# Odd layer: values stored by feature half, gate multiplied in the projection, sums of two heads at once, first projection tile emitted early; linear attention's second pass in backward order

## Chip, core and metric

The kernel runs on one core of a Trainium2 chip. The metric is the device time of one execution in microseconds (us). Before the change it is 3762.51 us, the median of 3 runs (3760.75 to 3772.91).

The core has TensorE (PE) for matrix products into PSUM, VectorE (DVE), ScalarE (ACT), GpSimd (POOL), and SyncE (SP), which here issues nearly all DMAs. Every engine works through its own queue in order. Where an instruction waits, all behind it on that engine wait too, the DMAs that SP or POOL are to issue included.

## What is computed

Two layers over 2048 latent tokens (a grid of 32 rows by 64 columns) and 256 context tokens, width 1024, in fp32. Layer 0 (even) has two branches, layer 1 (odd) has one:

```python
# layer 0: latent attention, 8 heads of 96 (values 64), keys = latents + context
s = q @ k.T * scale ; p = softmax(s) ; a = p @ v
# and gated linear attention, 4 heads, scanned over chunks in both directions
o = q_t @ state + att @ v ; state = state * decay + k_dec.T @ v
y = concat([a * silu(za), rms_norm(b) * silu(zb)]) @ w_out
# layer 1: neighbourhood attention, 16 heads of 64, window 8 rows x 16 columns
s = concat([q @ k_window.T * scale + bias, q @ k_ctx.T * scale])
o = softmax(s) @ concat([v_window, v_ctx])
y = (o * silu(z)) @ w_out
x = x + gate * y
```

## The kernel before

**Products.** fp32 operands are split into a high and a low fp32r part. A product is three matmuls: high x high, low x high, high x low (L114, L115, L116 in the projections; L961 to L963 in the even scores). L106 is the helper that every ACT instruction goes through.

**Stages**, by the trace: projections and row maxima of layer 0 to 1128 us; even attention with the linear attention woven into it, 1128 to 1993; projection 0 (18 tiles of 128 tokens) to about 2240; the four projections of layer 1 (`odd_qk`, `odd_vz`) to 3120; odd attention, 3120 to 3563; projection 1 (16 tiles) to the end, 3763.5.

**Even attention** (`even_attention`) runs 4 pairs of heads. For a block of up to 512 queries, it takes 18 key tiles of 128: scores on PE, exp on ACT into `apt`, `apt` times values on PE (L893). The sum of `apt` over the key tiles, the softmax's denominator before its last sum over partitions, is added up elementwise in `acc` (L952): two in five key tiles on POOL, the others on DVE, and L971 adds the two sums.

**Linear attention** (`gla`) has a first pass over 18 chunks, two scans (forward on POOL, tag gsf; backward on DVE, tag gsb: chunks 1, 0, then 17 down to 2, L788 to L790, three instructions for a chunk), and a second pass (L795 to L820) over chunks 0 to 17. The second pass multiplies the queries with the scanned states `D` (L804), adds, normalizes, transposes and copies the result with ACT into a tile of the tag gsb, which has two buffers and is also the scan's. `weave` puts its instructions into even attention's at a fixed ratio. When all is issued, the states' memory takes the split weights of projection 0 (the list `places`).

**Odd attention** (`odd_attention`) runs 8 pairs of heads j. For a pair, SP loads the queries (q, four tiles and a mask row), the context's keys (kc), two bias tables (tab; POOL adds the mask to each, L1338), the values V, and the latents' keys in four groups g of 512 tokens (kt), each ahead of its use. The two query sets of a pair are in fixed buffers, so that pair j+1's can be loaded when PE is through with pair j-1. Steps of a pair are c0, c1 (context keys for query blocks 0, 1), g0, c2, g1, c3, g2, g3. A group is four column tiles: scores (L1342, L1343), bias added on DVE from PSUM into `opt` (L1451), exp in place on ACT, then, some steps later, `opt` times values into the PSUM tile o (L1383; L1368 for context keys). The denominators are added up in `oacc`, per head: for context keys with a DVE reduce (L1374), for latent tiles with an add on POOL, for tiles 2 and 9 on DVE (L1391). `finish` sums over partitions on PE (L828), inverts on ACT and DVE, multiplies o by it (L835), multiplies by the gate z on POOL (L836; z is loaded by L1396), and a DMA of POOL's queue stores the block into RT1.

V is stored by POOL's DMAs (`store_v`) as 8 blocks of rows, one per residue of the grid row modulo 8. `values(j)` loads it back with one DMA for context rows (V1c) and eight for latents, of 16 partitions each: the 128 keys of a tile are in the order c, r, b (c: column group of 16, r: row modulo 8, b: column within 16), and so are K1t and the bias tables.

**Projection 1** (`project`): per tile, rows of RT (128 x 1024), hi on ACT, lo on DVE (L1066), 48 matmuls, gate (L1074) and residual (L1075). Its weights come in pair 7 in 16 chunks of 128 x 512 through one staging buffer (wraw, L375), are split by ACT and DVE (L378), and are placed in buffers that pairs 6 and 7 have left. Rows of tiles 0 and 1 are requested in between; PE takes their matmuls in the order in which the weights come.

The added instructions take their place on an engine from the order of emission, which `weave`, `issue_after` and a list of late steps move; nothing is planned by costs but the weave's ratio.

Of the kernel before, what the change touches and what calls it, by code (L numbers as in the profile page):

```python
# [17 lines left out]
P = 128  # L18
# [70 lines left out]
class Kern:  # L89
# [569 lines left out]

    def gla(self, gp, gs, g1, gd, pp, tag):  # L660
# [133 lines left out]
        scan(list(range(NCT - 1, -1, -1)) + list(range(NT - 1, NCT - 1, -1)), slice(64, 128), nc.vector, "gsb")  # L794
        for c in range(NT):  # L795
# [27 lines left out]
    def finish(self, av, dacc, zt, dst, w, ap, pp, tag, lnp=None, bufs=(1, 2), out=None):  # L823
# [12 lines left out]
        nc.gpsimd.tensor_tensor(out=rc[:, :w], in0=rc[:, :w], in1=zt, op=ALU.mult)  # L836
        (out or nc.sync).dma_start(dst, rc[:, :w])

    def even_attention(self, ap, pp):
# [71 lines left out]
        early, sums = {}, {}  # L911
        for j in range(4):
# [12 lines left out]
            for nb, (q0, w, kts) in enumerate(blocks):  # L925
# [8 lines left out]
                acc = [[None, None], [None, None]]  # L934
                first = [[None, None], [None, None]]

                def add(n, pts):
                    for i in range(2):
                        e = 1 if len(kts) > 2 and n % 5 in (1, 3) else 0
                        eng = nc.gpsimd if e else nc.vector  # L940
                        if acc[i][e] is None:
                            if first[i][e] is None:
                                first[i][e] = pts[i]
                                continue
                            if len(kts) == 2:
                                acc[i][e] = self.tl(ap, [P, CTX], f"accc{i}", bufs=1)
                            else:
                                acc[i][e] = self.tl(ap, [P, 512], f"acc{i}{e}", bufs=2 - e)
                            a = first[i][e]
                        else:  # L950
                            a = acc[i][e]
                        eng.tensor_tensor(out=acc[i][e][:, :w], in0=a[:, :w], in1=pts[i][:, :w], op=ALU.add)  # L952

                for n, kt in enumerate(kts):
# [13 lines left out]
                    if n == len(kts) - 1:  # L968
                        for i in range(2):
                            if acc[i][1] is not None:  # L970
                                nc.vector.tensor_tensor(out=acc[i][0][:, :w], in0=acc[i][0][:, :w], in1=acc[i][1][:, :w], op=ALU.add)  # L971
                        sums[j, nb] = [acc[i][0][:, :w] for i in range(2)]
# [19 lines left out]
    def even_mix(self, e1, win, hT):  # L992
# [3 lines left out]
        with ExitStack() as es:  # L996
            with ExitStack() as esa:
# [13 lines left out]
                places = [(g1, t) for t in ("gG", "gqt", "gkt", "gkT", "gat", "tri")] + [(gd, f"D{c}") for c in range(NT)]  # L1011
# [28 lines left out]
            self.project(0, self.RT, list(range(NT)), self.i["xin"], self.x1, w, sp, pp, ld, pre, ahead())  # L1040
# [4 lines left out]
    def project_load(self, RT, t, o, xsrc, ld):  # L1045
        r = self.tl(ld, [P, KD, P], "pr")
        self.nc.sync.dma_start(r[:], RT[:, :, o * P : o * P + P].rearrange("j p t -> p j t"))
# [4 lines left out]
    def project(self, l, RT, tiles, xsrc, dst, w, sp, pp, ld, pre, ahead=iter(())):  # L1052

        nc = self.nc
        gate = {}
        for c in range(2):
            if l == 0 or c == 0:
                gate[c] = self.tl(sp, [P, D], f"gate{c}", bufs=1)
                nc.sync.dma_start(gate[c][:], self.gates[l, c : c + 1].partition_broadcast(P))
        for t in tiles:  # L1060
            o = (t - tiles[0]) * P
            r, x = pre.pop(t) if t in pre else self.project_load(RT, t, t - tiles[0], xsrc, ld)
            hi = self.tl(sp, [P, KD, P], "prh", F32R)
            lo = self.tl(sp, [P, KD, P], "prl", F32R)
            self.act(hi[:], r[:])
            nc.vector.tensor_tensor(out=lo[:], in0=r[:], in1=hi[:], op=ALU.subtract)  # L1066
            g = gate[1 if t < NCT else 0]
            for n in range(2):
                c = slice(n * 512, n * 512 + 512)
                ps = self.tl(pp, [P, 512], "pj", bufs=4)  # L1070
                self.mm3(ps[:], (lambda k: hi[:, k, :], lambda k: lo[:, k, :]),
                         (lambda k: w[k, n][0][:, 0, :], lambda k: w[k, n][1][:, 0, :]), range(KD))
                y = self.tl(sp, [P, 512], "py")
                nc.vector.tensor_tensor(out=y[:], in0=ps[:], in1=g[:, c], op=ALU.mult)  # L1074
                nc.gpsimd.tensor_tensor(out=x[:, c], in0=y[:], in1=x[:, c], op=ALU.add)  # L1075
            nc.sync.dma_start(dst[o : o + P, :], x[:])
            next(ahead, None)
# [11 lines left out]
    def odd_qk(self, ws, win, hT):  # L1089
        nc = self.nc  # L1090
        self.V1c = self.scr("V1c", (P, NCT, D), F32)
        self.V1 = self.scr("V1", (8, 256, D), F32)
# [3 lines left out]
        with ExitStack() as es:  # L1096
# [8 lines left out]
            def cell(t, j):  # L1105
# [9 lines left out]
                if j == 4:  # L1115
                    n = self.tl(sp, [P, 512], "onat", bufs=4)
                    self.act(n[:], ps[:].rearrange("p h d -> p (h d)"))
                    self.store_v(t, slice(0, 512), n)
                    return
# [10 lines left out]
            def fin(t, j, n):  # L1130
# [24 lines left out]
                for r in range(2):  # L1155
                    oh, ol = (x[:].rearrange("p i (c r b) -> p i r c b", c=4, r=8)[:, :, r0 + r] for x in kt[j])
# [25 lines left out]
    def store_v(self, t, c, v):  # L1182

        if t < NCT:
            self.nc.gpsimd.dma_start(self.V1c[:, t, c], v[:])
            return
        g, a = divmod(2 * (t - NCT), 8)
        for r in range(2):
            self.nc.gpsimd.dma_start(self.V1[a + r, g * 64 : g * 64 + 64, c], v[r * 64 : r * 64 + 64])

    def odd_vz(self, ws, win, hT):
# [4 lines left out]
        with ExitStack() as es:  # L1196
# [6 lines left out]
            def cell(t, j):  # L1203
# [6 lines left out]
                if j < 6:  # L1210
                    self.act(n[:], ps[:])
                    self.store_v(t, slice((j - 4) * 512, (j - 3) * 512), n)
                    return
# [70 lines left out]
    def odd_attention(self, ld, right, wout):  # L1284
# [4 lines left out]
        with ExitStack() as es:  # L1289
# [51 lines left out]
            def scores(ps, k1, k2, q1, q2):  # L1341
                nc.tensor.matmul(ps, k1, q1, start=True, stop=False)  # L1342
                return nc.tensor.matmul(ps, k2, q2, start=False, stop=True)  # L1343

            mk = None
            pend, late = [], []
            for j in range(8):
# [15 lines left out]
                def tail_ctx(n, pts, j=j, V=V, O=O, acc=acc):  # L1363
# [6 lines left out]
                    for i in range(2):  # L1370
                        if n % 2 == 0:
                            acc[n // 2, i] = self.tl(rp, [P, 16, 64], f"oacc{n // 2}{i}", bufs=1)
                        a = acc[n // 2, i][:].rearrange("p r c -> p (r c)")[:, (n % 2) * 512 : (n % 2) * 512 + 512]
                        nc.vector.tensor_reduce(out=a, in_=pts[i][:].rearrange("p u c -> p c u"), axis=AX.X, op=ALU.add)  # L1374

                def tail(n, pts, j=j, V=V, O=O, acc=acc):
# [3 lines left out]
                    for bb in range(r0 // 8, (r0 + nr - 1) // 8 + 1):  # L1380
                        a0, a1 = max(r0, bb * 8), min(r0 + nr, bb * 8 + 8)
                        for i in range(2):
                            nc.tensor.matmul(O[bb][i * 64 : i * 64 + 64, a0 - bb * 8 : a1 - bb * 8, c0 : c0 + w],  # L1383
                                             V[:, NCT + n, i * 64 : i * 64 + 64], pts[i][:, a0 - r0 : a1 - r0, :],
                                             start=False, stop=bb in done, skip_group_check=True)
                    for hf in range(r0 // 16, (r0 + nr - 1) // 16 + 1):
                        a0, a1 = max(r0, hf * 16), min(r0 + nr, hf * 16 + 16)
                        for i in range(2):
                            a = acc[hf, i][:, a0 - hf * 16 : a1 - hf * 16, c0 : c0 + w]
                            eng = nc.vector if n in (2, 9) else nc.gpsimd  # L1390
                            eng.tensor_tensor(out=a, in0=a, in1=pts[i][:, a0 - r0 : a1 - r0, :], op=ALU.add)  # L1391
                    late.extend([2 + u, finish_block, bb, j, O, acc] for u, bb in enumerate(done))

                def finish_block(bb, j, O, acc):
                    zt = self.tl(fp, [P, 512], "ozt", bufs=3)
                    nc.sync.dma_start(zt[:], self.z1[j, :, bb * 512 : bb * 512 + 512])  # L1396
                    a = [acc[bb // 2, i][:].rearrange("p r c -> p (r c)")[:, (bb % 2) * 512 : (bb % 2) * 512 + 512] for i in range(2)]
                    self.finish(O.pop(bb)[:].rearrange("p r c -> p (r c)"), a, zt[:],
                                self.RT1[j, :, bb * 512 : bb * 512 + 512], 512, fp, pp, ("st", 4), lp, (2, 3), nc.gpsimd)

                def weights():

                    for k in range(KD):
# [5 lines left out]
                        elif k == 5:  # L1409
                            v = self.tl(vp, [P, NT, P], "ov", F32R)[:].rearrange("p t d -> p (t d)")  # L1410
# [11 lines left out]
                for kind, n in steps:  # L1422
                    g, c = divmod(n, 4)
                    exps = lambda: self.tl(ep, [P, 2, 512], "opt", bufs=5)
# [5 lines left out]
                    for i in range(2):  # L1430
# [22 lines left out]
                        self.act(pt, pt, AF.Exp)  # L1453
                    if kind == "l" and c == 3:
                        kt.pop(0)
                    if kind == "l":
                        pts = [pts[:, i, : nr * w].rearrange("p (r c) -> p r c", r=nr) for i in range(2)]
# [17 lines left out]
            for f, *a in pend:  # L1475
                f(*a)
            for _, f, *a in late:
                f(*a)

    def odd_tail(self, out):  # L1480
        with ExitStack() as es:
            qb, vp, lp, qa, kp, tp = [self.pool(es, "oa" + n, bufs=2, side="right", reuse_waits="tile") for n in ("QB", "V", "L", "QA", "KT", "T")]
            ld = self.pool(es, "wpX", bufs=2, side="left", reuse_waits="tile")
            w = {}
            att = self.odd_attention(ld, ((qa, qb), kp, tp, vp, lp), w)
            next(att)
            pre = {t: self.project_load(self.RT1, t, t - NCT, self.x1, ld) for t in range(NCT, NCT + 2)}
# [4 lines left out]
            self.project(1, self.RT1, list(range(NCT, NT)), self.x1, out, w, sp, pp, ld, pre)  # L1492
# [95 lines left out]
```

## Time and profile before

| | before |
|---|---|
| median of 3 runs | 3762.51 us |
| profiled execution | 3765.24 us |
| its span, first to last instruction | 3763.5 us |
| mean granted clock of TensorE | 0.977 |
| PE, DVE, ACT, POOL busy | 95%, 63%, 38%, 38% |
| even attention, 1131 to 1993 | PE busy 836 of 862 us |
| odd attention, pairs 2 to 6, 3240 to 3506 | PE busy 239 of 266 us, clock 0.94, DMA 0.91 |

The page gives busy time by engine, the chain of work that ended last, and groups of instructions by line. A row of instructions reads: engine, line, what is written and read, shapes, count, busy time and mean, and the idle time before them with its releaser. A row of a stretch reads: from and to, length, busy time and count for PE, weight loads, DVE, ACT and POOL, then granted clock, DMA share and GB/s. A row of waits reads: engine, line, waited for, total us, times, longest. The execution profiled is 2.7 us above the median.

### The profile page before, as it was taken

Reading aid. Unit: us, or ns where it says so; the run is one execution under the profiler, and the core shown is the slowest. Engines: PE = TensorE matmul, PEld = TensorE weight load, DVE = VectorE, ACT = ScalarE, POOL = GpSimd, SP = SyncE. Lnnn points to the kernel's source line nnn. Section 1 sums busy time; section 2 is a strip of 40 time slices with the busy share of each in tenths; the row PEclk is TensorE's granted clock in tenths of the full one; section 3 lists DMA queues with packets and bytes.
Section 4 is the critical chain, followed back from the end, with each engine's and each line's share of the span. In section 5 each row is a group of like instructions: output and inputs, shape, how many; then the busy total and the mean of one; then the engine's idle time right before and its main releaser. Section 6 shows DMA issues by size and latency. Waiting matters only on the chain.

```text
span 3763.5 us, 52191 instructions
## 1 busy us (share of the span) xinstructions
PE 3585.0 (95%) x18404; PEld 2760.9 (73%) x18404; DVE 2373.4 (63%) x4731; ACT 1441.5 (38%) x2868; POOL 1436.7 (38%) x1669
## 2 busy tenths in 40 slices
PE   7999989999999999998999999999999998889899
PEld 6988978888886666655657878887788885555577
DVE  4677656888866556696654344445687764667732
ACT  4445541111125555545552134444322223555510
POOL 1434320010124444455542233333344334776722
PEclk9999999999999999999999999999999998999899
DMA  7455463222242231424515545545544449898543
GB/s 255 137 164 159 129 171 93 77 85 75 77 133 66 85 95 57 121 80 124 154 51 168 166 145 148 148 142 177 192 133 140 137 107 219 191 221 202 159 143 118
DMA packets 355415, 512.28 MB, mean 136 GB/s; under 512 B 27105, under 2 KB 229937, under 8 KB 349250
## 3 DMA queue, kind: packets, MB, share of 16 engines
q1 hardware_dynamic: 312786, 425.56, 40.4%
q0 software_dynamic: 19712, 55.40, 5.0%
q10 hardware_dynamic: 22656, 27.99, 2.1%
q8 instruction: 146, 2.39, 0.3%
q14 instruction: 115, 0.94, 0.1%
HBM read 329.45 MB, written 179.37 MB: 135 GB/s over the span
## 4 chain that ended last, share of the span: by engine, by line
PE 74%; DMA 12%; DVE 6%; issue 3%; POOL 3%; ACT 2%; SPq 0%; POOLq 0%; ACTq 0%; DVEq 0%
PE gm L123 9%; PE gm L124 9%; PE gm L125 9%; PE av L893 6%; PE st L961 4%; PE mx L646 4%; PE pj L116 3%; PE pj L114 3%; PE pj L115 3%; PE st L962 3%; PE st L963 3%; DMA q<-Q 2%; DMA wraw<-w_od 2%; DMA ov<-V 1%; DMA kt<-K1t 1%
## 5 line engine op out<-in xcount | busy, mean ns | idle before, releaser
L106 ACT ACTIVATE apt<-st 128x512 f32<-128x512 f32 (+1 forms) x592 | 343.8, 593 | 280.0 <-PE st L963 250.8
L647 DVE TENSOR_REDUCE mm<-mx 128x1 f32<-128x512 f32 (+1 forms) x656 | 389.0, 627 | 82.0 <-PE mx L646 75.0
L952 DVE TENSOR_TENSOR acc<-acc,apt 128x512 f32<-128x512 f32 x288 | 276.3, 983 | 142.4 <-ACT apt L106 140.8
L952 POOL TENSOR_TENSOR acc<-acc,apt 128x512 f32<-128x512 f32 x160 | 224.9, 1419 | 195.3 <-ACT apt L106 194.8
L893 PE MATMUL av<-apt,av 128*64 128x512 f32 (+1 forms) x1184 | 278.5, 594 | 0.0
L961 PE MATMUL st<-aq,akh 97*128 97x512 f32 (+1 forms) x592 | 255.0, 431 | 9.2 <-ACT apt L106 7.2
L646 PE MATMUL mx<-mk,mq 96*128 96x512 f32 (+1 forms) x656 | 236.9, 373 | 6.4 <-DMA mq<-QT 4.9
L962 PE MATMUL st<-aq,akh 96*128 96x512 f32 (+1 forms) x592 | 233.5, 395 | 0.0
L963 PE MATMUL st<-aq,akl 96*128 96x512 f32 (+1 forms) x592 | 233.0, 394 | 0.0
L1391 POOL TENSOR_TENSOR oacc<-oacc,opt 128x341 f32<-128x341 f32 (+6 forms) x336 | 213.3, 664 | 47.0 <-ACT opt L106 39.9
L1265 DVE CUSTOM_DVE_ANT_1 mx<-mx,mtab 128x225 f32<-128x225 f32 (+13 forms) x576 | 183.6, 338 | 57.4 <-PE mx L1259 42.1
L106 ACT ACTIVATE u<-gm 128x352 f32<-128x352 f32 (+1 forms) x140 | 68.6, 497 | 372.6 <-PE gm L125 208.5
L1075 POOL TENSOR_TENSOR px<-py,px 128x512 f32<-128x512 f32 x68 | 90.8, 1336 | 286.9 <-DVE py L1074 267.9
L1451 DVE TENSOR_TENSOR opt<-st,tab 128x64 f32<-128x64 f32 (+10 forms) x576 | 145.1, 313 | 78.0 <-PE st L1343 46.7
L893 PEld LDWEIGHTS av<-apt,av 128*64 128x64 f32 x1184 | 80.2, 137 | 152.3 <-issue 150.8
L106 ACT ACTIVATE opt<-opt 128x465 f32<-128x465 f32 (+7 forms) x256 | 124.5, 504 | 160.6 <-DVE opt L1451 141.6
L961 PEld LDWEIGHTS st<-aq,akh 97*128 97x128 f32 x592 | 111.8, 189 | 96.7 <-issue 46.1
L1074 DVE TENSOR_TENSOR py<-pj,gate 128x512 f32<-128x512 f32 x68 | 46.8, 690 | 205.9 <-PE pj L116 205.4
L646 PEld LDWEIGHTS mx<-mk,mq 96*128 96x128 f32 x656 | 121.7, 189 | 17.9 <-issue 5.3
L963 PEld LDWEIGHTS st<-aq,akl 96*128 96x128 f32 x592 | 112.8, 191 | 25.1
L106 ACT ACTIVATE prh<-pr 128x1024 fp32r<-128x1024 f32 x34 | 35.7, 1056 | 241.5 <-PE pj L115 237.8
L962 PEld LDWEIGHTS st<-aq,akh 96*128 96x128 f32 x592 | 113.3, 191 | 16.9
(444 smaller groups left out, 10284.5 us busy)
## 6 DMA issues: line engine op xcount, KB each, us to landing
q<-Q SPq DMA_DIRECT2D x48, 512.0 KB
H<-x ACTq DMA_DIRECT2D x36, 512.0 KB
pr<-RT SPq DMA_DIRECT2D x34, 512.0 KB
adaw<-ada_w SPq DMA_DIRECT2D x64, 256.0 KB
x<-H SPq DMA_DIRECT2D x32, 512.0 KB
wraw<-w_od SPq DMA_DIRECT2D x64, 256.0 KB
K1t<-okt POOLq DMA_DIRECT2D x32, 512.0 KB, 7.3
kt<-K1t SPq DMA_DIRECT2D x32, 512.0 KB
```

The costliest lines, as they stand in the source:

```text
L106: return self.nc.scalar.activation(out, in_, func, **kw)
L123: self.nc.tensor.matmul(out, lh(k), rh(k), start=j == 0, stop=False)
L124: self.nc.tensor.matmul(out, lh(k), rl(k), start=False, stop=False)
L125: self.nc.tensor.matmul(out, ll(k), rh(k), start=False, stop=j == n - 1)
L646: mm = nc.tensor.matmul(ps[:, :w], q[:A_QK, (t % 6) * P : (t % 6) * P + P], k[:A_QK, k0 : k0 + w], start=True, stop=True)
L647: nc.vector.tensor_reduce(out=m[:, t, n : n + 1], in_=ps[:, :w], axis=AX.X, op=ALU.max)
L893: nc.tensor.matmul(O[j, nb][i * 64 : i * 64 + 64, :w], V[j, kt // TT][:, kt % TT, i * 64 : i * 64 + 64], pts[i][:, :w], start=n == 0, stop ...
L952: eng.tensor_tensor(out=acc[i][e][:, :w], in0=a[:, :w], in1=pts[i][:, :w], op=ALU.add)
L961: nc.tensor.matmul(ps[:, :w], kh[: A_QK + 1, i, kq], qh[: A_QK + 1, :w], start=True, stop=False)
L962: nc.tensor.matmul(ps[:, :w], kh[:A_QK, i, kq], ql[:A_QK, :w], start=False, stop=False)
L963: mm = nc.tensor.matmul(ps[:, :w], kl[:A_QK, i, kq], qh[:A_QK, :w], start=False, stop=True)
L1391: eng.tensor_tensor(out=a, in0=a, in1=pts[i][:, a0 - r0 : a1 - r0, :], op=ALU.add)
```

## The change

1. The second pass of the linear attention, and the list of places for weights, go through the chunks in the backward scan's order.
2. In even attention all sums are on DVE, in one accumulator for each head. The 192 adds of POOL move, the 32 combining adds go.
3. In odd attention `finish` gets no gate; the 32 loads and POOL products go. Projection 1 loads z beside each tile's rows (512 KB) and multiplies on POOL in place.
4. V is stored by feature half, with latents in their natural order; `values(j)` is one DMA for context rows and one of 128 partitions for latents. The keys of a tile are in the order c, b, r, and `odd_qk` writes them with a stride of 8 elements.
5. `opt` holds both heads: one exp, one add (on POOL for all tiles) per key tile. The context sums of even blocks go to POOL. `opt` has 6 buffers (5).
6. Projection 1's first tile is issued within odd attention's end, with attention's tiles and PSUM banks, ahead of the last denominators on PE; its second half stands before the other tiles.

```diff
-        for c in range(NT):
+        for c in self.back_order():
...
-        nc.gpsimd.tensor_tensor(out=rc[:, :w], in0=rc[:, :w], in1=zt, op=ALU.mult)
+        if zt is not None:
+            nc.gpsimd.tensor_tensor(out=rc[:, :w], in0=rc[:, :w], in1=zt, op=ALU.mult)
...
                 def add(n, pts):
                     for i in range(2):
-                        e = 1 if len(kts) > 2 and n % 5 in (1, 3) else 0
-                        eng = nc.gpsimd if e else nc.vector
...
+                        if n == 0:
+                            first[i] = pts[i]
+                        else:
+                            a = first[i] if n == 1 else acc[i]
+                            nc.vector.tensor_tensor(out=acc[i][:, :w], in0=a[:, :w], in1=pts[i][:, :w], op=ALU.add)
...
-                places = [(g1, t) for t in ("gG", "gqt", "gkt", "gkT", "gat", "tri")] + [(gd, f"D{c}") for c in range(NT)]
+                places = [(g1, t) for t in ("gG", "gqt", "gkt", "gkT", "gat", "tri")] + [(gd, f"D{c}") for c in self.back_order()]
...
+    def project_load(self, RT, t, o, xsrc, ld, z=None, zp=None):
+
+        load = lambda src: self.nc.sync.dma_start(r[:], src[:, :, o * P : o * P + P].rearrange("j p t -> p j t"))
+        if z is not None:
+            f = r = self.tl(zp or ld, [P, KD, P], "pr")
+            load(z)
         r = self.tl(ld, [P, KD, P], "pr")
+        load(RT)
         x = self.tl(ld, [P, D], "px")
         self.nc.sync.dma_start(x[:], xsrc[t * P : t * P + P, :])
+        if z is not None:
+            self.nc.gpsimd.tensor_tensor(out=r[:], in0=r[:], in1=f[:], op=ALU.mult)
         return r, x
...
-        self.V1c = self.scr("V1c", (P, NCT, D), F32)
-        self.V1 = self.scr("V1", (8, 256, D), F32)
+        self.V1c = self.scr("V1c", (2, P, NCT, 512), F32)
+        self.V1 = self.scr("V1", (2, SEQ, 512), F32)
...
-                    oh, ol = (x[:].rearrange("p i (c r b) -> p i r c b", c=4, r=8)[:, :, r0 + r] for x in kt[j])
+                    oh, ol = (x[:].rearrange("p i (c b r) -> p i r c b", c=4, r=8)[:, :, r0 + r] for x in kt[j])
...
             def values(j):
-                V = self.tl(vp, [P, NT, P], "ov")
-                c = slice(j * P, j * P + P)
-                nc.sync.dma_start(V[:, :NCT, :], self.V1c[:, :, c])
-                for a in range(8):
-                    nc.sync.dma_start(V[a * 16 : a * 16 + 16, NCT:, :], self.V1[a, :, c].rearrange("(n b) d -> b n d", b=16))
+                V = self.tl(vp[j % 2], [P, NT, P], "ov", bufs=1)
+                f, c = j // 4, slice(j % 4 * P, j % 4 * P + P)
+                nc.sync.dma_start(V[:, :NCT, :], self.V1c[f, :, :, c])
+                nc.sync.dma_start(V[:, NCT:, :], self.V1[f].rearrange("(n p) d -> p n d", p=P)[:, :, c])
                 return V
...
+                    for i, a in enumerate(sums(acc, n)):
                         if n % 2 == 0:
...
+                            nc.gpsimd.tensor_tensor(out=a, in0=pts[i][:, 0, :], in1=pts[i][:, 1, :], op=ALU.add)
+                        else:
+                            nc.vector.tensor_reduce(out=a, in_=pts[i][:].rearrange("p u c -> p c u"), axis=AX.X, op=ALU.add)
...
-                        for i in range(2):
-                            a = acc[hf, i][:, a0 - hf * 16 : a1 - hf * 16, c0 : c0 + w]
-                            eng = nc.vector if n in (2, 9) else nc.gpsimd
-                            eng.tensor_tensor(out=a, in0=a, in1=pts[i][:, a0 - r0 : a1 - r0, :], op=ALU.add)
+                        a = acc[hf][:, :, a0 - hf * 16 : a1 - hf * 16, c0 : c0 + w]
+                        nc.gpsimd.tensor_tensor(out=a, in0=a, in1=pts[:, :, a0 - r0 : a1 - r0, :], op=ALU.add)
...
                 def finish_block(bb, j, O, acc):
-                    zt = self.tl(fp, [P, 512], "ozt", bufs=3)
-                    nc.sync.dma_start(zt[:], self.z1[j, :, bb * 512 : bb * 512 + 512])
...
-                        self.act(pt, pt, AF.Exp)
...
+                        pts = pts[:, :, : nr * w]
+                        self.act(pts, pts, AF.Exp)
...
             next(att)
-            pre = {t: self.project_load(self.RT1, t, t - NCT, self.x1, ld) for t in range(NCT, NCT + 2)}
+            t = NCT
+            rows, x = self.project_load(self.RT1, t, 0, self.x1, ld, self.z1)
+            next(att)
+            ap, fp, ps, g = self.lent
+            g = self.gate_load(1, 0, g[:].rearrange("p i c -> p (i c)").bitcast(F32))
+            first = self.project_tile(rows, x, self.tl(ap, [P, KD, P], "prh", F32R, bufs=1)[:],
+                                      self.tl(ld, [P, D], "px", F32R)[:].rearrange("p (k t) -> p k t", k=KD), g, w,
+                                      lambda: self.tl(ps, [P, 512], "st", bufs=4), lambda: self.tl(fp, [P, 512], "rc", bufs=3), out[:P, :])
+            next(first)
+            next(att)
+            for _ in first:
+                pass
             for _ in att:
                 pass
...
-            self.project(1, self.RT1, list(range(NCT, NT)), self.x1, out, w, sp, pp, ld, pre)
+            self.project(1, self.RT1, [(t, t - NCT) for t in range(NCT + 1, NT)], self.x1, out, w, sp, pp, ld, {}, [g], self.z1)
```

More of the change, by code (lines that the diff above doesn't have):

```diff
@@ L793, in gla @@
         scan(list(range(NT)), slice(0, 64), nc.gpsimd, "gsf")
[L794 to L795 removed]
+        scan(self.back_order(), slice(64, 128), nc.vector, "gsb")
+        for c in self.back_order():
             qT = self.tl(gs, [P, H, P], "gqT")
@@ L909, in step_late @@
             late[:] = [x for x in late if x[0] > 0]
-        early, sums = {}, {}
+        early, sums, first = {}, {}, {}
         for j in range(4):
@@ L968, in even_attention @@
                     if n == len(kts) - 1:
-                        for i in range(2):
-                            if acc[i][1] is not None:
-                                nc.vector.tensor_tensor(out=acc[i][0][:, :w], in0=acc[i][0][:, :w], in1=acc[i][1][:, :w], op=ALU.add)
-                        sums[j, nb] = [acc[i][0][:, :w] for i in range(2)]
+                        sums[j, nb] = [a[:, :w] for a in acc]
                     pend.append((j, nb, n, kt, pts))
@@ L1054, in project @@
         nc = self.nc
[L1055 to L1076, printed above, removed]
@@ L1343, in scores, with sums @@
                 return nc.tensor.matmul(ps, k2, q2, start=False, stop=True)
+            def sums(acc, bb):
+                return [acc[bb // 2][:, i].rearrange("p r c -> p (r c)")[:, (bb % 2) * 512 : (bb % 2) * 512 + 512] for i in range(2)]
             mk = None
```

90 lines of the change are left out of this document (53 added, 37 removed).

## The prediction

> **What bounds the kernel now.** I read the busy table first, then the table by stages, then PE's waits in the two stages where it stops, then the chain there. The page:
>
> ```profile
> PE 3585.0 (95%) x18404; PEld 2760.9 (73%) x18404; DVE 2373.4 (63%) x4731; ACT 1441.5 (38%) x2868; POOL 1436.7 (38%) x1669
> PE 74%; DMA 12%; DVE 6%; issue 3%; POOL 3%; ACT 2%; SPq 0%; POOLq 0%; ACTq 0%; DVEq 0%
> ```
>
> TensorE carries the time, with DMA behind it. Where it does not is read from the stretches (columns: from:to, length, then busy us and instructions of PE, PEld, DVE, ACT, POOL; granted clock, DMA share, GB/s):
>
> ```profile
> 1131.00:1617.00 486.00, 482.48 (x2504) 305.13 (x2503) 304.90 (x362) 264.34 (x533) 227.22 (x194) 1.00 0.30 84
> 1617.00:1690.00 73.00, 67.34 (x292) 40.60 (x291) 70.27 (x74) 35.00 (x61) 38.56 (x25) 0.98 0.32 89
> 1690.00:1720.00 30.00, 15.18 (x65) 9.61 (x66) 21.19 (x32) 10.97 (x26) 5.95 (x6) 0.72 0.13 36
> 1720.00:1993.00 273.00, 271.03 (x1239) 160.79 (x1238) 166.95 (x199) 152.42 (x304) 149.21 (x122) 1.00 0.39 109
> ...
> 3240.00:3506.00 266.00, 238.71 (x1522) 142.69 (x1520) 187.19 (x489) 140.34 (x280) 189.86 (x261) 0.94 0.91 206
> 3506.00:3563.00 57.00, 52.09 (x330) 31.32 (x328) 46.27 (x113) 34.47 (x71) 40.24 (x57) 0.94 0.52 147
> ```
>
> Even attention (1131 to 1993) keeps PE full, but for the backward scan: there DVE is busy 70.27 of 73 us, and then PE stands. The timeline shows on what:
>
> ```profile
> 1702.90 0.69 DVE L789 TENSOR_TENSOR gsb<-gsb,D 64x512 f32<-64x512 f32 x1
> 1703.62 1.14 ACT L106 ACTIVATE gsb<-gl,gn 128x128 f32<-128x128 f32 x4 [15.11 <-DVE gsb L789]
> ...
> 1704.82 2.07 PE L804 MATMUL gl<-D,gqT 128*128 128x128 f32 x8 [14.84 <-ACT gsb L106]
> ```
>
> The copy of the first second-pass chunk (ACT, tile gsb, two buffers shared with the scan) waits for the last scan step on DVE. Until then its PSUM bank gl is held, and PE's third L804 with it. That is a buffer, not the order of the chunks.
>
> Odd attention (3120 to 3563, eight head pairs j) has DMA at 0.91. A pair lasts 59.7, 60.2, 51.5, 52.5, 56.4, 51.8, 54.0 and 57.3 us (between first kc scores). PE's waits in pairs 2 to 6, the two longest (total us, times, longest; a second wait for kt, at L1343, has 2.1 more), then the chain at the start of pair 3:
>
> ```profile
> PE st L1342 <- DVE opt L1451: 13.0, 21, 2.4
> PE st L1342 <- DMA kt<-K1t: 9.4, 4, 4.5
> ```
>
> ```profile
> 3289.18 5.05 DMA q<-Q
> ...
> 3294.25 15.05 DMA q<-Q
> ...
> 3309.32 9.64 DMA ov<-V
> ...
> 3319.02 8.43 DMA kt<-K1t
> ```
>
> A pair's start frees the query buffers; SP then sends q, two tables, V and only behind them this pair's own third key group. These 38 us of queue end later than PE wants the keys; after each such gap the clock is 0.54 to 0.83 for some 10 us.
>
> **The change, part by part.**
>
> *Even attention, all sums on DVE.* 192 adds move to it and 32 combining adds go: 544 are left, 288+32 were there. A DVE add takes 0.69 us when POOL is idle (142 of the 288) and about 1.27 beside POOL; the mean is
>
> ```profile
> L952 DVE TENSOR_TENSOR acc<-acc,apt 128x512 f32<-128x512 f32 x288 | 276.3, 983 | 142.4 <-ACT apt L106 140.8
> L952 POOL TENSOR_TENSOR acc<-acc,apt 128x512 f32<-128x512 f32 x160 | 224.9, 1419 | 195.3 <-ACT apt L106 194.8
> ```
>
> With POOL's adds gone, 544 x 0.69 = 375 us against some 331 now (288 and 32 first adds, and the combines). Spread over 862 us, with DVE busy 563 of them, +44 is covered by PE; at the bad end, 544 x 0.983 = 535, DVE is busy 767 of 862 and still covered outside the scan. 0, with ±5.
>
> *The scan stretch.* From the first second-pass add to the scan's end the DVE order holds 88 instructions before (78.5 us, 0.89 each) and 116 after, because the moved adds join it. At 0.70 to 0.74, 116 take 82 to 86 us. PE's work queued ahead of the stalled matmul grows from 57.1 to 71.9 us (counted by columns, 0.224 us per 512). So the excess falls from 85.2 - 57.1 = 28 to about 12 us (10 to 14): **-14** after rounding down for the clock. At 0.89 an add it is 103 - 72 = 31, +3; if the stall goes whole, -28. The back order moves neither the buffer nor the third L804, which stays behind the scan's end: 0 by itself, and the weight places D follow it.
>
> *Odd attention, loads.* V's packets of 512 B take 46 to 92 ns (mean 60 in pair 3's queue), 16 partitions a load; V1c's and the projection's rows, 512 B too but on 128 partitions, take 27 to 30. A V is 2304 packets: 2304 x 60 / 16 = 8.6 us becomes 3.9 if the new single load is like these, which I take, as source pitch (4 to 8 KB) and packet size are the same. At the worst nothing is gained. The gate's load (131 ns per 2048 B packet, 1.05 us per 256 KB) leaves the queue four times a pair, twice ahead of the keys: 2 us. The queue shrinks from 38 to about 31 us, while PE reaches the third group in 32: the 11.5 us of key waits and the cold clock go (0.94 over 266 us is 16 us at most).
>
> [...]
>
> *Odd attention, engines.* DVE per pair goes from 41 to about 32 us: six adds leave (0.58 each) and four of eight context reduces (L1374, 1.24), and less. Four half sums move to POOL (1.16 each by its fit of 0.19 us + 1.9 ns per element on L1391: 5.1 us), with the six adds (3.8); merging saves about 4 in fixed costs and the gate's product 5.4: POOL stays near 34 us, plus about 9 in which its table add waits for the DMA. ACT has half the calls. Against 13.0 us of waits for L1451 this gains a part. What is left is the pace of stretches without stalls, 48 us (c0, c1, g0: 16; c2, g1: 12.5; c3, g2, g3: about 20), not the 39.7 us of PE columns. Pairs 2 to 6: 53.2 - 48 = 5.2 each, **-26**. Pair 1, at 60 with 6.0 us for keys and 8.4 for the finish of pair 0: 50, **-10**. Pair 0: V now stands ahead of kc, mask and second q, some 10 us of PE start lost (2.6 MB at 203 GB/s are 12.8 us behind the last store of values), but its 4.6 us for V1c and 1.3 for V go and the rest catches up on what has landed: **0**, -5 to +8.
>
> The gain needs POOL and DVE not to slow each other: L1451 reads PSUM and one table and shows no change beside POOL.
>
> *Strided key stores.* ACT 468 and DVE 480 ns, 64 each; doubled they are 60 us beside a stage in which PE is full (2240 to 3120): 0.
>
> *Pair 7, transition.* PE has a 9.06 us gap at 3572.6: POOL's gate product (3558.4), RT store 5.80, load 4.12, hi copy 1.07. The product goes from there, but comes back on 128x1024 (about 2.5 us, from the 128x1034 POOL add, 2.39). Behind it stands another limit: 16 weight chunks pass one staging buffer, at least 2.65 (DMA) + 0.63 + 0.69 + issue = 4.2 us each, 3505.6 to 3595.4, and before, tiles 0 and 1 were both done at 3597.8, interleaved as weights came. After, twelve chunks stand ahead of tile 0's rows on SP, four behind loads that wait for its product; only tile 0 is run while they land, and tile 1 (10.9 us) follows. From pair 7's start: 12 chunks by about +58, the last at +75, tile 0 done at +77, tile 1 at +88, against +91.6 now. **-4**, -8 to +12.
>
> *Project 1.* 512 KB more per tile (1024 packets x 28 / 16 = 1.8 us of 10.9) at a DMA share of 0.43, POOL +2.5 us per tile at a quarter busy, loads issued two tiles ahead: 0. Without that cover, 15 x 2.5 = +38.
>
> Sum: -14 - 10 - 26 - 4 = -54. The profiled execution is 3765.2 us (its span of 3763.5 and 1.7 around it): 3711. It lies 2.7 above the median of the runs shown, so **3709**.
>
> **Rivals.**
> 1. *V gets no faster.* The queue shrinks by the gate's 2 us only, half the key waits stay: pairs 2 to 6 -12, pair 1 -5, scan -14, transition -2: 3730. For it: other loads run in the same queue, and V's packets may be slow only for being in it. Against: 27 ns for V1c beside them. 0.2.
> 2. *PE alone is the bound.* With DVE relieved and the queue short, pairs reach 44 us (39.7 of columns and the sums): 5 x 9.2 + 16 for pair 1 + 28 for the scan = 90: 3672. Against: 48 where nothing stalls. 0.15.
> 3. *POOL takes DMA's place in odd attention*, slower than before. It is in order; the table adds wait for DMA at its head, and the sums ahead of finish and of the RT stores stand behind. Its 34 + 9 + 5 (tables, issue) is 48 a pair already. At 1.22 times (1419 over 1163 by the fit, as L952 has beside DVE) the pair is 55, at 1.3 times 58: pairs 2 to 6 +24, pair 0 +8 (its late start uncaught), pairs 1 and 7 -1, scan -14: +17, 3780. It decides from about 57 a pair, 1.26 times. Against: two-input DVE adds leave this stage. 0.11.
> 4. *No change*: the transition costs its +12, project 1's products show, pair 0 loses 8, and pairs keep 51: within 11 us. 0.07.
>
> Forecast 0.47. The range 3660 to 3756 takes in rivals 1 and 2 and a part of 4, and leaves out 3. A measurement of this kernel tells 0.3%, 11 us, from no change: faster 0.82, within 0.07, slower 0.11.
>
> **What would show it.** V's packets at 27 to 30 ns and no wait of PE for kt in pairs 2 to 6; pairs of 47 to 49 us; DVE adds near 0.69 us, and one L804 wait of 10 to 14 us, still released by gsb; tile 1 done some 88 us after pair 7's start. It is wrong if PE waits for POOL's oacc (rival 3), if pairs stay above 51, or if project 1's tiles take more than 10.9 us.

## The result

The changed kernel takes 3750.68 us against 3769.20 us before (medians of 12 runs each): a ratio of 0.9954, interval 0.9943 to 0.9966, some 17 us less. The forecast was 54 us less. The profiled execution takes 3754.91 us; its span is 3753.1 us, 10.4 below that of before, and it lies 4 us above its median as that of before lies 4 below the median of these 12. So the profiles show about 7 us less of a difference than the runs.

Of the page after, the busy table and the chain by engine:

```profile
PE 3585.8 (96%) x18404; PEld 2767.6 (74%) x18404; DVE 2356.7 (63%) x4843; ACT 1436.6 (38%) x2740; POOL 1217.0 (32%) x1349
...
PE 76%; DMA 10%; DVE 5%; POOL 4%; issue 3%; ACT 2%; SPq 1%; POOLq 0%; ACTq 0%; DVEq 0%
```

POOL has lost 220 us of work, and yet its share of the chain has grown from 3 to 4%. The stretches that answer to those of before:

```profile
1131.00:1617.00 486.00, 482.94 (x2501) 306.47 (x2500) 332.58 (x467) 266.39 (x536) 104.98 (x99) 1.00 0.30 87
1617.00:1690.00 73.00, 72.51 (x303) 42.56 (x303) 70.79 (x104) 35.83 (x62) 8.37 (x7) 0.95 0.25 69
1690.00:1720.00 30.00, 26.78 (x119) 17.31 (x120) 22.30 (x33) 17.95 (x42) 6.68 (x7) 0.89 0.35 104
...
3226.60:3485.80 259.20, 233.48 (x1523) 140.43 (x1521) 149.52 (x441) 126.63 (x200) 193.06 (x172) 0.94 0.74 192
3485.80:3543.60 57.80, 51.28 (x322) 31.59 (x320) 39.42 (x100) 33.30 (x54) 38.75 (x35) 0.88 0.45 139
```

The scan's stretch is filled (PE 72.51 of 73 us, and 26.78 of 30 where it was 15.18). In pairs 2 to 6 DMA fell from 0.91 to 0.74 and DVE from 187 to 150 us, but the five pairs take 259.2 us after 266.0, and the clock is still 0.94. Marks of the two profiles:

| us | before | after | gain up to here |
|---|---|---|---|
| first matmul of projection 0 | 1999.2 | 1986.3 | 12.9 |
| first score of pair 0 | 3120.1 | 3117.9 | 2.2 |
| of pair 1 | 3179.8 | 3176.0 | 3.8 |
| of pair 2 | 3240.0 | 3226.6 | 13.4 |
| of pair 7 | 3506.2 | 3485.8 | 20.4 |
| end | 3763.5 | 3753.1 | 10.4 |

So three places fall short: the way to pair 0 (10.7 us lost), pairs 2 to 6 (7 gained, 26 forecast), and what follows pair 7's start (10 lost, 4 forecast as gain).

What stops PE in pairs 2 to 6 now, from the waits of PE, then DVE, then POOL:

```profile
PE st L1346 <- DVE opt L1456: 22.3, 20, 3.0
```

```profile
DVE opt L1456 <- POOL oacc L1399: 52.9, 19, 4.9
```

```profile
POOL tab L1342 <- DMA tab<-rpb_k: 40.8, 5, 8.8
```

No wait for kt is left (11.5 us before). PE waits for DVE's bias adds (22.3 us, 13.0 before), these wait for POOL's sums (52.9, 22.6 before), and POOL waits for the bias tables of the next pair, about 8 us a pair as before. The timeline of pair 2 has it in order:

```profile
3246.24 4.76 POOL L1342 TENSOR_TENSOR tab<-tab,maskk 128x1034 f32<-128x1034 f32 x2 [7.16 <-DMA tab<-rpb_k]
...
3250.95 1.64 POOL L1399 TENSOR_TENSOR oacc<-oacc,opt 128x744 f32<-128x744 f32 x1
...
3252.62 1.19 DVE L1456 TENSOR_TENSOR opt<-st,tab 128x465 f32<-128x465 f32 x2 [3.30 <-POOL oacc L1399]
...
3256.81 1.07 DVE L1456 TENSOR_TENSOR opt<-st,tab 128x240 f32<-128x240 f32 x4 [3.00 <-POOL oacc L1399]
...
3257.54 0.47 PE L1346 MATMUL st<-q,kc 128*128 128x512 f32 x1 [2.93 <-DVE opt L1456]
```

POOL stands 7.16 us for the tables and then works 4.76 on them. The sums behind it give the exp buffers back late, DVE has no buffer to write, and PE no PSUM bank.

### The profile page after: what moved, and what is told of

The parts are those of the page before. It is cut to its first block, busy times and chain, and to the rows that moved or that the text cites. A ratio compares the mean times of both kernels' runs of the same rounds, so it can differ in the third digit from the quotient of the medians.

```text
span 3753.1 us, 51813 instructions
## 1 busy us (share of the span) xinstructions
PE 3585.8 (96%) x18404; PEld 2767.6 (74%) x18404; DVE 2356.7 (63%) x4843; ACT 1436.6 (38%) x2740; POOL 1217.0 (32%) x1349
## 4 chain that ended last, share of the span: by engine, by line
PE 76%; DMA 10%; DVE 5%; POOL 4%; issue 3%; ACT 2%; SPq 1%; POOLq 0%; ACTq 0%; DVEq 0%
PE gm L123 9%; PE gm L124 9%; PE gm L125 9%; PE av L899 7%; PE st L957 4%; PE mx L646 4%; PE st L958 4%; PE st L959 4%; PE pj L116 3%; PE pj L114 3%; PE pj L115 3%; DMA tab<-rpb_k 2%; DMA wraw<-w_od 2%; PE o L1393 1%; PE gm L114 1%
## 5 line engine op out<-in xcount | busy, mean ns | idle before, releaser
L948 DVE TENSOR_TENSOR acc<-acc,apt 128x512 f32<-128x512 f32 x512 | 365.0, 738 | 154.4 <-ACT apt L106 151.4
L1399 POOL TENSOR_TENSOR oacc<-oacc,opt 128x528 f32<-128x528 f32 (+5 forms) x192 | 217.7, 1157 | 46.0 <-ACT opt L106 44.7
L106 ACT ACTIVATE opt<-opt 128x930 f32<-128x930 f32 (+7 forms) x128 | 103.4, 808 | 187.0 <-DVE opt L1456 184.3
L123 PE MATMUL gm<-w1h,hhi 128*128 128x512 f32 x288 | 116.9, 406 | 7.1 <-ACT onat L106 7.1
L106 ACT ACTIVATE x<-px,modB,modA 128x128 f32<-128x128 f32 x272 | 99.1, 468 | 58.5 <-PE px L326 39.7
```

The costliest lines, as they stand in the source:

```text
L106: return self.nc.scalar.activation(out, in_, func, **kw)
L123: self.nc.tensor.matmul(out, lh(k), rh(k), start=j == 0, stop=False)
L948: nc.vector.tensor_tensor(out=acc[i][:, :w], in0=a[:, :w], in1=pts[i][:, :w], op=ALU.add)
L1399: nc.gpsimd.tensor_tensor(out=a, in0=a, in1=pts[:, :, a0 - r0 : a1 - r0, :], op=ALU.add)
```

## Experiments

Each ratio is to the kernel before on the same chip, with its interval. Theory A: the place of the table adds in POOL's queue, with more sums behind them, has taken the place of DMA. Theory B: POOL has too much work. Theory C: PE's own pace sets it. Theory T is for the transition to projection 1. The name in brackets is the run's.

**Tables late** (tab_late)

```diff
-                nc.gpsimd.tensor_tensor(out=tb[:], in0=tb[:], in1=mk[:], op=ALU.add)
+                with self.tc.issue_after(mark[0].ins) if mark else ExitStack():
+                    nc.gpsimd.tensor_tensor(out=tb[:], in0=tb[:], in1=mk[:], op=ALU.add)
...
-                        nc.gpsimd.tensor_tensor(out=a, in0=a, in1=pts[:, :, a0 - r0 : a1 - r0, :], op=ALU.add)
+                        add = nc.gpsimd.tensor_tensor(out=a, in0=a, in1=pts[:, :, a0 - r0 : a1 - r0, :], op=ALU.add)
+                    if n == 5:
+                        mark[:] = [add]
```

> The changed kernel, but POOL's two mask adds on the next pair's bias tables stand behind the sums of key tile 5 in POOL's queue, ten rows later than before; nothing else moves. Theory A: pairs 2 to 6 stay at 51.8 us because POOL stands at the head of its queue for those tables (40.8 us in five pairs), the sums behind it hold the exp buffers, and DVE waits for these (52.9 us). Then POOL's wait for tab falls below 8 us, DVE's wait for POOL's sums below 25, pairs 2 to 6 take 48 to 49.5 us, and the time is 12 to 22 us below the changed kernel. Theory B: POOL has too much work (193 of 259 us busy) and a later place only moves the stop: pairs stay at 51 to 52.5, the time within 6 us. Theory C: PE's own pace (cold clock 0.94) sets it: DVE's waits for POOL fall, pairs stay.

Measured: 0.9875 (0.9858 to 0.9892), 30 us below the changed kernel, more than either theory gave. Pairs 2 to 6 in its profile:

```profile
3210.10:3438.40 228.30, 220.82 (x1522) 135.05 (x1520) 149.67 (x441) 126.67 (x200) 194.15 (x171) 1.00 0.83 218
```

POOL does as much as before (194 us) and waits for no table, DVE for no sum of POOL, and a pair takes 45.7 us at a clock of 1.00. The place in the queue is what cost, not the work: B falls as stated, and so does C, since the pairs became shorter.

**Sums back on DVE** (sums_dve)

```diff
-                        if n % 2 == 0:
-                            nc.gpsimd.tensor_tensor(out=a, in0=pts[i][:, 0, :], in1=pts[i][:, 1, :], op=ALU.add)
-                        else:
+                        if True:
                             nc.vector.tensor_reduce(out=a, in_=pts[i][:].rearrange("p u c -> p c u"), axis=AX.X, op=ALU.add)
...
-                        nc.gpsimd.tensor_tensor(out=a, in0=a, in1=pts[:, :, a0 - r0 : a1 - r0, :], op=ALU.add)
+                        (nc.vector if n in (2, 9) else nc.gpsimd).tensor_tensor(out=a, in0=a, in1=pts[:, :, a0 - r0 : a1 - r0, :], op=ALU.add)
```

> The changed kernel, but the context sums of even blocks and the sums of tiles 2 and 9 are on DVE, as they were before the change (about 8 us less on POOL and 9 more on DVE per pair); the tables stay where they are in POOL's queue. Theory A (the head of POOL's queue): POOL still waits about 40 us for tables in pairs 2 to 6; fewer sums stand behind it, so DVE's waits for it fall from 52.9 to 25 to 40, and pairs take 50 to 51.5 us (51.8). Theory B (too much work on POOL): pairs fall to 49 us or less, 12 us or more in all.

Measured: 0.9878 (0.9862 to 0.9893), pairs of 46.0 us, with POOL's wait for the tables still there:

```profile
POOL tab L1342 <- DMA tab<-rpb_k: 29.4, 5, 6.3
```

That is the figure stated for theory B, and A as stated missed: moving the work cures it as well as moving the tables does. Both together read so: the stop reaches PE only when it meets a POOL that has too many sums behind it to catch up before the exp buffers run out. The stop alone was there before the change (44.4 us in pairs 2 to 6), with fewer sums behind it (DVE waited 22.6 us for them), beside the waits for the DMA.

**Both cures** (late_dve): tables late and sums back.

> The changed kernel with both cures of odd attention: tables late (tab_late) and context sums and tiles 2 and 9 on DVE (sums_dve). If each alone already leaves PE the only bound of a pair (45.5 to 46 us at full clock), the two do not add: pairs 45.3 to 46.5, the time within 6 us of tab_late (ratio 0.986 to 0.989). If each cures a different half, pairs fall below 44.5 and the time by 8 us or more below tab_late.

Measured: 0.9861 (0.9845 to 0.9877), pairs of 45.6 us. They do not add: PE, busy 220.9 of 228.2 us in pairs 2 to 6, is the bound of a pair at about 45.6 us.

**Five exp buffers** (opt5)

```diff
-                    exps = lambda: self.tl(ep, [P, 2, 512], "opt", bufs=6)
+                    exps = lambda: self.tl(ep, [P, 2, 512], "opt", bufs=5)
```

> The changed kernel with 5 exp buffers (opt) in place of 6. If POOL's stop at the tables reaches PE through the exp buffers that the sums behind it hold, one buffer fewer fills earlier: PE's waits for DVE in pairs 2 to 6 grow from 22 us to 35 to 55 and pairs from 51.8 to 53.5 to 57 us, 10 to 30 us in all. If the buffers are not the link, pairs stay within 1 us.

Measured: 0.9936 (0.9922 to 0.9950), which overlaps with the changed kernel's interval, so that no difference in time can be told; the 10 to 30 us more that were expected did not come. In the profile pairs take 49.4 us, shorter by 2.4, and PE's waits for DVE fall to 14.9 us. In its timeline DVE has one long wait a pair, 4.8 to 6.0 us, for the first sum behind the tables; with six buffers it waits three or four times, in pair 2 for 3.30, 3.00 and 2.13 us, the second time for a sum that has a store and two context sums ahead of it. So the buffers look like the link, and which sum a buffer waits for counts for more than their number. This is read from two timelines; no run isolates it.

**V's form alone** on the kernel before (part 4 of the change).

```diff
-                for a in range(8):
-                    nc.sync.dma_start(V[a * 16 : a * 16 + 16, NCT:, :], self.V1[a, :, c].rearrange("(n b) d -> b n d", b=16))
+                nc.sync.dma_start(V[:, NCT:, :], self.V1[f].rearrange("(n p) d -> p n d", p=P)[:, :, c])
```

> The kernel before with part 4 alone: values by feature half, V in one load of 128 partitions, the tile's keys in the order c, b, r. If the load's form makes V slow (theory), its 512 B packets fall from 62 ns to about 32, as in the changed kernel, PE's waits for kt in pairs 2 to 6 fall from 11.5 us to under 4, and pairs take 50 to 52 us (53.2), 8 to 16 us in all with pair 1. If the queue was not what held the pairs (rival: DVE waiting for POOL's sums, 22.6 us, takes the place at once), they stay within 1 us of 53.2 and the time within 6 us.

Measured: 0.9948 (0.9935 to 0.9961), 20 us alone; pairs of 50.9 us, no wait for kt in pairs 2 to 6, 25.0 us of DVE's waits for POOL's sums left. V's 512 B packets take 33 ns here and in the changed kernel (62 before).

**The gate alone** (part 3).

```diff
-        nc.gpsimd.tensor_tensor(out=rc[:, :w], in0=rc[:, :w], in1=zt, op=ALU.mult)
+        if zt is not None:
+            nc.gpsimd.tensor_tensor(out=rc[:, :w], in0=rc[:, :w], in1=zt, op=ALU.mult)
...
+        if z is not None:
+            self.nc.gpsimd.tensor_tensor(out=r[:], in0=r[:], in1=f[:], op=ALU.mult)
```

> The kernel before with part 3 alone: no gate in attention, z loaded and multiplied in projection 1, tiles 0 and 1 loaded within attention as before. If POOL's place in attention is what counts (theory A), its 20 products and their waits for DVE go (L836 waited 17.1 us for DVE in pairs 2 to 6), DVE waits less for POOL's sums (22.6 us before) and the queue loses two 256 KB loads ahead of the keys: pairs 2 to 6 take 50.5 to 52.5 us (53.2), 4 to 14 us in all with pair 1; less what the products cost between attention and projection 1 (0 to 6). If the gate in attention was covered, pairs stay within 0.5 us and the time is the same or up to 6 us longer.

Measured: 0.9969 (0.9957 to 0.9981), 12 us. Pairs take 49.0 us, 4.2 less each, though V is as slow as before (64 ns a packet) and PE still waits 6.4 us for kt: DVE's waits for POOL's sums fell to 13.7 us. That is more than was foreseen. From pair 7's start to the end it takes 264.7 us against 257.3.

**Even attention's two parts**, each alone on the kernel before.

```diff
-                        e = 1 if len(kts) > 2 and n % 5 in (1, 3) else 0
-                        eng = nc.gpsimd if e else nc.vector
...
+                            nc.vector.tensor_tensor(out=acc[i][:, :w], in0=a[:, :w], in1=pts[i][:, :w], op=ALU.add)
```

> The kernel before with part 2 alone: all sums of even attention on DVE. Theory: these sums alone make the gain at the scan, because more of PE's work stands ahead of the stalled L804 and the adds are short; PE's wait at L804 falls from 14.8 us to 3 to 6, DVE adds to about 0.73 us, the time by 9 to 16 us. Rival: the order of the second pass makes it; then the wait stays above 10 us and the time within 5 us.

Measured: 0.9966 (0.9955 to 0.9978), 13 us; the wait at L804 is 3.89 us.

```diff
-        for c in range(NT):
+        for c in self.back_order():
```

> The kernel before with part 1 alone: second pass and weight places in backward order. Theory: the wait is for the scan's two gsb buffers, whatever chunk comes first: 13 to 16 us at L804 as before, time within 5 us. Rival (the order is what helps): wait under 6 us, time 8 us or more lower.

Measured: 0.9998 (0.9987 to 1.0009); the wait is 15.10 us. The order alone does nothing; the sums do it.

**The transition.** Without the early first tile:

```diff
-            first = self.project_tile(rows, x, self.tl(ap, [P, KD, P], "prh", F32R, bufs=1)[:],
...
+            pre = {t: self.project_load(self.RT1, t, t - NCT, self.x1, ld, self.z1) for t in range(NCT, NCT + 2)}
```

> The changed kernel without the early first tile: rows of tiles 0 and 1 are loaded within attention as before the change, with one buffer more for z, their products on POOL, and PE takes both tiles' matmuls as the weights come. Theory T: tile 1 is late in the changed kernel (second half done at +103 us from pair 7's start, +92 before the change) because only tile 0 runs while the weights land, and tile 1's product stands behind tile 0's residual adds on POOL. Then both tiles are done at +88 to +95 and the time is 6 to 14 us below the changed kernel. Rival: what costs is the product itself and z's load, wherever the tile stands: within 4 us of the changed kernel.

Measured: 0.9937 (0.9922 to 0.9951), some 6 us below the changed kernel, with intervals that overlap. From pair 7's start to the end: 261.9 us (267.3 in the changed kernel, 257.3 before). Tiles 0 and 1 are done at +98, not at +88 to +95, so theory T is met in part.

With tile 1's product on DVE:

```diff
-            self.nc.gpsimd.tensor_tensor(out=r[:], in0=r[:], in1=f[:], op=ALU.mult)
+            (self.nc.vector if o == 1 else self.nc.gpsimd).tensor_tensor(out=r[:], in0=r[:], in1=f[:], op=ALU.mult)
```

> The changed kernel, but tile 1's product with the gate (and tile 1's of projection 1 alone) is on DVE in place of POOL. Theory T: PE's gap of 7.98 us ahead of tile 1 comes from POOL's order (product behind tile 0's second residual add, which ends at 3571.3); on DVE it comes behind tile 0's second gate product (ends 3569.8) and takes 1.2 us in place of 2.4: the gap falls to 4 to 5 us, the time by 3 to 4. Rival: z's load (issued at 3561.9 behind the last weight chunk) or the row copies end last: gap 7 to 8 us, no change.

Measured: 0.9949 (0.9935 to 0.9963), no difference that can be told. The product took 2.12 us on DVE, not 1.2; the gap went from 7.98 to 5.79 us, but another of 1.26 follows, for tile 1's low part on DVE. To the end it is 266.8 us.

With tables late and tile 1's rows early:

```diff
+            f1 = self.tl(ep, [P, KD, P], "opt", bufs=6)
+            self.nc.sync.dma_start(f1[:], self.z1[:, :, P : 2 * P].rearrange("j p t -> p j t"))
...
+            self.nc.gpsimd.tensor_tensor(out=r1[:], in0=r1[:], in1=f1[:], op=ALU.mult)
             next(first)
```

> The changed kernel with the tables' mask adds late (as in tab_late) and tile 1's rows ready early: its z is loaded into a free exp buffer ahead of the last three weight chunks, and its product stands on POOL ahead of tile 0's residual adds. Theory T: in tab_late, PE's gap ahead of tile 1 is 7.55 us and tile 1's second half is gated at +101 us from pair 7's start; then the gap goes (under 2 us), tile 1 is done at +91 to +95, and the time is 6 to 9 us below tab_late's ratio of 0.9875, 0.985 to 0.986. Rival: the weights' chain slips by what is put ahead of it, and tile 1 ends within 3 us of tab_late's.

Measured: 0.9875 (0.9859 to 0.9892), as tab_late. In the profile the gap ahead of tile 1 is 0.5 us and the way from pair 7's start 260.9 us (265.2), but pair 2 took 51.2 us, for a wait of 2.6 us for kt.

Tables late, without the early tile (late_nofirst):

> tab_late without the early first tile (tiles 0 and 1 as in no_first). If the early tile as the change makes it costs time whatever attention does, tile 1 is done at +96 to +99 from pair 7's start (101 in tab_late) and the time is 3 to 6 us below tab_late. If no_first only gained because attention was slow, there is no gain or a loss of up to 3 us.

Measured: 0.9863 (0.9849 to 0.9877), 262.4 us to the end (265.2 in tab_late), with one pair of 50.7 us, for a wait of 3.6 us for kt. The five kernels with a cure of attention, 0.9861 to 0.9878, cannot be told apart; each is some 46 to 52 us below the kernel before and some 29 to 35 below the changed one.

## Why the prediction was wrong, step by step

**Added up**, the parts alone give -13 (sums), -20 (V), -12 (gate) and 0 (order): -45. The change gives -17. If the parts add, which no run shows, what is left of it, merged sums, their move to POOL and the early tile, costs 28. Taking the move back alone brings 29. The early tile costs 3 to 8 in the profiles: from pair 7's start to the end, the five kernels with it as the change makes it take 265.2 to 269.5 us, the two without it 261.9 and 262.4.

**Right.** The scan: -14 forecast, 12.9 in the profile, 13 alone. The size of the change was right, its level was not: from the first to the third L804 PE stood 20.5 us before and 5.3 after, where the prediction had an excess of 28 and 12, too much by about 7 both times. So the stall left at L804 is 3.7 us, not 10 to 14. The mean of the adds is 0.74 us, between the 0.69 without POOL beside them and the 1.27 with it:

```profile
L948 DVE TENSOR_TENSOR acc<-acc,apt 128x512 f32<-128x512 f32 x512 | 365.0, 738 | 154.4 <-ACT apt L106 151.4
...
1693.22 2.08 PE L809 MATMUL gl<-D,gqT 128*128 128x128 f32 x8 [3.71 <-ACT gsb L106]
```

The back order at 0. V's packets came to the rate of the 128-partition loads, and the waits for kt went. (The new rows of V lie 2 KB apart, not 4 to 8; it did no harm.) The Trainium skill, "SBUF — State Buffer", section "Door 1", gives 104 GB/s for 16 partitions and 328 for 128. The trace agrees in kind: 512 B on 16 engines in 62 ns are 132 GB/s, in 33 ns 248. PE's pace in projection 1 is unchanged, 11.2 us a tile before and after, so the sign of being wrong, more than 10.9, lay below what the kernel took already. Pair 0, 0: 1.6.

**Right by luck.** Pair 1, -10: 9.6. It still holds 3.1 us of waits for DVE, and without the stop it takes 45.3 us (tab_late), not the 50 of the forecast: two errors cancel.

**Wrong: pairs 2 to 6, -26 forecast, -7 measured.** The step that failed is "POOL stays near 34 us, plus about 9 in which its table add waits for the DMA". It counted POOL's time and not its order; the time itself was right (193 us in five pairs, tables included, 190 before). The stop begins some 12 us into a pair, and the change puts all sums that release the exp buffers behind it: also the six tile sums and half of the context sums, which DVE had done and which a stop of POOL could not hold. The sum of the forecast has no term for that. Rival 3 named the engine and the sums behind its head, but by a price (POOL slowed 1.22 times by DVE) that was not seen (the 744-element add took 1.63 us, 1.60 by the fit; the 512-element context sum 1.28, 1.16 by the fit), and a threshold of 57 us a pair, from the sum of its work; it bit at 51.8. DVE's 41 us a pair was the sum of its groups; its busy time went from 37.4 to 29.9.

The pace was wrong in the other direction: 48 us was read from stretches that still held waits and cold clock, and without stops it is 45.6. With the queue cured, rival 2 was nearly right for the pairs.

**Wrong: the transition, -4 forecast, +10 measured.** The mis-sized term is tile 1, at +88 in the sum. PE was through it at +103 (+91.6 before); +10 lies within the stated -8 to +12. PE now stands twice, for tile 0's rows as before (9.1 us then), and again for tile 1's:

```profile
PE st L114 <- ACT prh L106: 8.9, 1, 8.9
PE pj L114 <- ACT prh L106: 8.0, 1, 8.0
```

The weights were in time, but POOL's order was not seen:

```profile
3566.24 1.30 POOL L1065 TENSOR_TENSOR px<-rc,px 128x512 f32<-128x512 f32 x1 [15.48 <-DVE rc L1064]
...
3570.02 1.28 POOL L1065 TENSOR_TENSOR px<-rc,px 128x512 f32<-128x512 f32 x1
...
3571.83 4.66 POOL L1050 TENSOR_TENSOR pr<-pr,pr 128x1024 f32<-128x1024 f32 x2
...
3575.32 0.80 PE L114 MATMUL pj<-wo0h,prh 128*128 128x512 f32 x1 [7.98 <-ACT prh L106]
```

Tile 1's product stands behind both residual adds of tile 0, which stand behind the last weights. While these land PE has one tile to work on where it had two. That this order makes the second stop is read from the trace, and the kernel with tile 1's rows early, where the stop is 0.5 us, bears it out; no difference in time was clear of noise. Of the loss, between half and three quarters is the product and z's load (the gate alone: +7.4 in this place; without the early tile: +4.6).

**Open.** Between projection 0 and pair 0 the profiles lose 10.7 us. 5.8 is one wait for the first queries, which pair 0's term of 0 was to cover; the nine kernels built on the changed one have it, 4.9 to 6.6 us, and the other five do not. No cure of attention touches it. Some 2.6 us is a second wait at the start of projection 0, in the ten kernels with even attention's sums all on DVE, and in no other (1.7 to 2.6). The rest is many small waits that differ from run to run: the kernel with the gate alone loses 10.7 us here too, and the runs of one kernel spread over 15 to 20 us. No run was made for any of it.

## What to carry to other kernels

When work moves to an engine that has time to spare, look for the longest wait in its queue and count what now stands behind it and who holds a buffer for that; busy time did not show it here (POOL 193 us of pairs 2 to 6 with the loss, 194 without). A transfer that is made shorter shows the next wait behind it, so add the sum again with the queue gone. And an early first tile gained nothing here, where the tile after it had its inputs prepared behind the first one's results.

## What the runs showed of the hardware

A short stop of PE can cost more than its length, since the granted clock falls after it. In the kernel with both late tables and early rows, pair 2 waits 2.05 and 0.57 us for kt and takes 51.2 us, pair 3 without such a wait 45.7. The stretches after that wait (granted clock is the third figure from the end):

```profile
3246.00:3248.00 2.00, 1.48 (x5) 1.41 (x6) 0.72 (x3) 0.00 (x0) 0.31 (x1) 0.57 0.67 146
...
3250.00:3252.00 2.00, 2.00 (x12) 0.94 (x10) 0.07 (x1) 0.98 (x1) 2.00 (x2) 0.50 0.03 8
...
3255.00:3258.00 3.00, 3.00 (x32) 1.79 (x31) 1.56 (x6) 1.84 (x3) 1.20 (x2) 1.00 0.53 152
```

Some 7 us at half speed follow 2.6 us of waiting, and the pair loses 5.5. In the kernel with late tables and no early tile one pair waits 2.98 and 0.64 us for kt, 3.4 us at a clock of 0.50 follow, and it takes 50.7 us where the others take 45.3 to 46.0: 5 lost for 3.6. Not every stop has this price: in tab_late a stop of 2.00 us at 3478 is followed by a clock of 1.00. No run here shows what decides it.

The Trainium skill, "TensorE: Matmul & The Clock Gate", Part 1, puts the fall at an idle window of about 3.4 us; here shorter stops were enough. By that rule stops under 3 us would cost only themselves. In pairs 2 to 6 of the changed kernel none is longer than 3.0 us, and against the kernel with both cures (51.8 and 45.6 us a pair) they cost more: 3.7 us a pair are PE standing (25.7 against 7.3 us in five pairs), and 2.5 are slower matmuls at a clock of 0.94 (PE busy 233.5 against 220.9 us with as many matmuls).
